# Normed tiles in places of their own, and another order of the seven MLP products, in a two-layer hybrid transformer kernel

## The chip, the cores and the metric

The kernel runs on one NeuronCore of one Trainium2 chip. The metric is the device time of one execution in microseconds (us); lower is better. A profiled execution gives a trace of each engine's instructions: PE (matrix engine), DVE (vector engine), ACT (scalar engine), POOL (the GpSimd engine) and SP (which issues most of the DMAs).

## The reference

Two layers work on x, 512 tokens by 1024 features in float32. Each layer norms x, projects it, mixes it in three ways (retention, sparse attention over keys that an indexer picks, dilated attention), projects back and adds to x; then it norms x again and adds an MLP. A last norm gives the output.

```
for layer in range(2):
    h = rms_norm(x, attn_norm_w[layer])
    proj = h @ w_in[layer]
    mixed = concat(retention(proj), dsa(proj), dilated(proj))
    x = x + mixed @ w_out[layer]
    h = rms_norm(x, mlp_norm_w[layer])
    x = x + square(relu(h @ w_up[layer])) @ w_down[layer]
return rms_norm(x, final_norm_w)
```

Here `rms_norm(x, w) = x * rsqrt(mean(x*x) + 1e-6) * w`, over the 1024 features of one token.

## The kernel before, in words

**Tiles.** x lies in four token tiles t = 0..3 (`xv`, 128 tokens by 1024 features). Every matrix product is made in float32r from a high and a low part of both operands, as three matmuls (high by high, high by low, low by high). A weight is loaded raw by DMA, ACT casts its high part (L277), and DVE or POOL subtracts to get the low part (L285); the pair is a `w` tile, and there are 5 buffers for those.

**A norm of one token tile** (`norm`): POOL multiplies one half of x by the norm's weights (L383), ACT squares and sums both halves (L360), DVE joins the two sums (L363), POOL raises to the power -0.5 (L367), DVE multiplies the first half by that (L387) and makes the second half in one instruction (L390). PE turns each half in 4 transposes (L351, 4 of 128x128 into an `at` bank). From there ACT casts the high part of the activations (L400), and DVE subtracts for the low part (L401), 256 columns at a time. The two normed halves and the two junk outputs of the squares all come from one pool, `P`, of 3 buffers of 128x512, which the sparse attention's small tiles use too.

**Start of a layer.** `token_parts` multiplies the activations of each token tile by a 456-column piece of `w_in` (L347, 24 matmuls for a token tile, 96 in all); then the indexer's matmuls follow (L335 with 128x384). At the start of layer 0 the norm's weights are spread over the partitions by two matmuls into PSUM (L1071), and two copies on ACT (L1086) bring them into a tile `ph` after the norm of tile 2, which reads them in PSUM. `attention` also zeroes two tiles: the retention state `sv` in four DVE instructions (L833) and the low parts of the keys, `KL`, in four POOL ones (L837).

**The MLP** of a layer goes through four stages f = 0..3, each a quarter of the 4096 hidden features: 8 blocks of up-projection (L335, 24 matmuls each), and then the down-projection in seven Strassen-like products P1 to P7. Each product has two parts p = 0, 1 of 12 matmuls of 128x512 (L1032) and two `w` tiles; a first part and a second part add to different token tiles. The products gather in PSUM banks that are not cleared between them (`CHAIN`): P1, P6, P7 and P4 follow each other in the two `rt` banks, P5 and P3 in two `at` banks, P2 stands alone. After each part, one DVE instruction (L1036) adds the bank to half of a token tile of x; the next product of the chain can only write to the bank once that add has read it. P1, P6, P3 and P2 go to tiles 0 and 1, P5, P7 and P4 to tiles 2 and 3; P4 and P2 add to the first half of the features, P6, P7, P5 and P3 to the second. In the last stage of a layer, `finish` starts the norm of a token tile that is complete (layer 0: the next layer's norm; layer 1: `final`, which writes the output).

**What sets the order.** The order on each engine is set before the run by a scheduler that simulates engines and takes a table of priorities; within an engine, instructions run in that order. Weight DMAs are issued ahead by SP as raw buffers come free.

Of the kernel before, what the change touches and what calls it, by code (L numbers as in the profile page):

```python
# [41 lines left out]
PRODUCTS = (("P1", 0), ("P5", 3), ("P6", 4), ("P2", 1), ("P7", 5), ("P3", 6), ("P4", 2))  # L42
# [5 lines left out]
FINISH = ({("P4", 0): (0,), ("P4", 1): (1, 2, 3)},  # L48
          {("P3", 0): (0,), ("P4", 0): (2,), ("P3", 1): (1,), ("P4", 1): (3,)})
# [33 lines left out]
O_PW = O_G + 2  # L83
N_C0 = O_PW + 8
# [9 lines left out]
def constants():  # L94
    f = np.float32
    c = np.zeros((P, N_CST), f)
    i = np.arange(P)
    c[:, O_ID:O_ID + 128] = np.eye(P, dtype=f)
    for k in range(NT):
        d = k * P + i[:, None] - i[None, :]  # L100
        n = ((d >= 0) & (d <= 128)).astype(int) + ((d >= 0) & (d % 4 == 0)) + ((d >= 0) & (d % 16 == 0))
        m = np.where(n > 0, -np.log(np.maximum(n, 1)), BIG)
        o = O_DIL + (NT - 1 - k) * P
        c[:, o:o + P] = m.astype(f)
    d = i[:, None] - i[None, :]
# [12 lines left out]
    c[:, O_PW:O_PW + 8] = -0.5  # L118
    return c
# [7 lines left out]
class Kern:  # L127
    UB = 5

    def __init__(self, nc, tc, ctx, A, out):  # L130
        self.nc, self.tc, self.A, self.out = nc, tc, A, out
        pool = self.pool


        self.psm = pool(ctx, "sm", 9)
        self.p1 = pool(ctx, "const", 1)
        self.pact = pool(ctx, "act", 4)
        self.praw = pool(ctx, "raw", RAWB)
# [215 lines left out]
    def norm_stats(self, t, junk=None, cuts=((0, 512), (512, 1024))):  # L354
# [12 lines left out]
        nc.gpsimd.tensor_tensor(r[:, 0:1], v[:, 0:1], self.c[:, O_PW:O_PW + 1], op=ALU.pow)  # L367
# [7 lines left out]
    def norm(self, t, wb, act, first=False, junk=None, h0=0):  # L375

        nc = self.nc
        hn = [None, None]
        hn[h0] = self.work()
        halves = ((0, 512), (512, 1024))[::1 - 2 * h0]  # L380
        if not first:
            c0, c1 = halves[0]
            nc.gpsimd.tensor_tensor(hn[h0], self.x[t][:, c0:c1], wb[:, c0:c1], op=ALU.mult)  # L383
        r = self.norm_stats(t, junk, halves)
        for h in (h0, 1 - h0):
            if h == h0 and not first:
                nc.vector.tensor_scalar(hn[h], hn[h], r[:, 0:1], None, op0=ALU.mult)  # L387
            else:
                hn[h] = hn[h] or self.work()
                nc.vector.scalar_tensor_tensor(hn[h], self.x[t][:, h * 512:(h + 1) * 512], r[:, 0:1],  # L390
                                               wb[h] if first else wb[:, h * 512:(h + 1) * 512], op0=ALU.mult,
                                               op1=ALU.mult)
            ps = self.at()
            for k in range(4):
                self.tr(ps[:, k * P:(k + 1) * P], hn[h][:, k * P:(k + 1) * P])
# [150 lines left out]
    def token_parts(self, L, act):  # L546
# [5 lines left out]
        for t in (0, 1, 2, 3) if L else (2, 3, 0, 1):  # L552
# [96 lines left out]
    def ret_tile(self, L, t, mix):  # L649
# [83 lines left out]
        nc.gpsimd.tensor_tensor(var[:, 4:8], var[:, 0:4], self.c[:, O_PW:O_PW + 4], op=ALU.pow)  # L733
# [12 lines left out]
    def latent(self, L, c):  # L746
# [10 lines left out]
        nc.gpsimd.tensor_tensor(ss[:, 4:8], ss[:, 0:4], self.c[:, O_PW:O_PW + 4], op=ALU.pow)  # L757
# [65 lines left out]
    def attention(self, L, act):  # L823
# [11 lines left out]
        for z in range(4):  # L835
            o = slice(64, 128) if z % 2 == 0 else slice(0, 64)
            nc.gpsimd.tensor_scalar(self.kl[z // 2][o, z % 2, :], bc(self.ident[o], [[0, 4], [1, P]]), 0.0, 0.0, op0=ALU.mult, op1=ALU.add)  # L837
# [98 lines left out]
        for t in range(NT):  # L936
# [3 lines left out]
            with self.prio("norm", t):  # L940
                self.norm(t, wb, nact)
# [3 lines left out]
    def mlp(self, L, act):  # L945
# [4 lines left out]
        with ExitStack() as ctx:  # L950
# [4 lines left out]
            psw = self.pool(ctx, "wb%d" % L, 1)  # L955

            U = pu.tile([P, 14 * 1024 + 64 * L], F32R, name="U%d" % L)[:, 64 * L:].rearrange("p (j f k c) -> p j f k c", j=2, f=7, k=4)
            for f in range(4):
# [44 lines left out]
                def finish(t):  # L1003
# [4 lines left out]
                    else:  # L1008
                        self.norm(t, wb, nact, h0=t // 2)
# [3 lines left out]
                if L == DEPTH - 1 and last:  # L1013
                    seq[-3:-1] = seq[-2:-4:-1]
                bank = {}
                for key, fac, p in seq:
# [20 lines left out]
                    for t in FINISH[L].get((key, p), ()):  # L1037
                        finish(t)
# [4 lines left out]
    def final(self, t, wb, pool, junk):  # L1043
        nc = self.nc
        h0 = t // 2
        halves = [(0, 512), (512, 1024)][::1 - 2 * h0]
# [3 lines left out]
        r = self.norm_stats(t, junk, halves if t < 3 else halves[:1] + [(d0, d0 + 256), (d0 + 256, d1)])  # L1050
# [6 lines left out]
    def start(self):  # L1057
# [7 lines left out]
        nc.sync.dma_start(self.c[:, :N_C0], self.A["cst"][:, :N_C0])  # L1065
        one = self.work()
# [15 lines left out]
        for t, n in zip((2, 3, 0, 1), PRE):  # L1082
            self.norm(t, wps if t == 2 else wb, act, t == 2)
            if t == 2:
                for h in range(2):
                    nc.scalar.copy(wb[:, h * 512:(h + 1) * 512], wps[h])  # L1086
# [40 lines left out]
```

## Time and profile before

| what | us |
|---|---|
| device time, three runs | 1262.68, 1267.45, 1267.89 (median 1267.45) |
| device time of the profiled execution | 1265.72 |
| span of its trace | 1263.8 |
| PE busy | 1221.3 (97%) |
| DVE busy | 924.7 (73%) |
| ACT busy | 677.6 (54%) |
| POOL busy | 466.6 (37%) |

The span goes from the first to the last instruction in the trace; the device time has a little around it (here 1.92 us). An engine's busy time is summed over the span. Since one engine is busy for almost all of the time, the page's averages say little about the rest: what a change can save is read from the stretches in which that engine stands still or runs slower, and from what it waits for there.

### The profile page before, as it was taken

To read this page: it belongs to the slowest core of one execution; us is meant where nothing else is said; L and a number is where in the kernel's file an instruction comes from. 1 tells how busy PE (TensorE), PEld (TensorE's weight loads), DVE (VectorE), ACT (ScalarE), POOL (GpSimd) and SP (SyncE) were. 2 spreads that over 40 slices of the span, in tenths; PEclk is the share of its full clock that TensorE was granted. 3 is DMA by queue.
4 is the path that set the end of the run, shared out by engine and by line. 5 is a ranking of instruction groups with operands and counts; after the bars stand their busy time and mean duration, and the time that the engine had idled before them with its cause. 6 is when DMAs were issued, how large, how long until landed. Compare 5 with 4: busy or idle time off the path is not lost.

```text
span 1263.8 us, 16891 instructions
## 1 busy us (share of the span) xinstructions
PE 1221.3 (97%) x6116; PEld 1033.1 (82%) x6116; DVE 924.7 (73%) x1589; ACT 677.6 (54%) x1241; POOL 466.6 (37%) x459
## 2 busy tenths in 40 slices
PE   7989999999999999999989999999999999999997
PEld 5978888878888888888879788888798888888886
DVE  6499757856884966858856996586678759578595
ACT  5646558734644535445446465676355445454454
POOL 2444648543411404114024445565444032041232
PEclk9999999999999999999989999999899999999999
DMA  7423223224435062250134232232161531614201
GB/s 211 117 67 92 79 72 118 68 66 130 137 111 157 1 207 59 80 167 16 45 116 134 76 97 71 68 118 66 51 223 45 176 91 44 189 34 140 77 1 67
DMA packets 142180, 122.73 MB, mean 97 GB/s; under 512 B 6801, under 2 KB 114065, under 8 KB 142098
## 3 DMA queue, kind: packets, MB, share of 16 engines
q1 hardware_dynamic: 140178, 118.52, 31.2%
q10 hardware_dynamic: 1920, 3.15, 1.1%
q8 instruction: 48, 0.79, 0.3%
q14 instruction: 34, 0.28, 0.1%
HBM read 114.31 MB, written 4.19 MB: 94 GB/s over the span
## 4 chain that ended last, share of the span: by engine, by line
PE 78%; DVE 15%; ACT 2%; issue 2%; DMA 1%; POOL 1%; SPq 0%; POOLq 0%; DVEq 0%; ACTq 0%
PE mm L335 33%; PE mm L347 14%; PE rt L1032 13%; PE at L1032 9%; DVE sc L604 3%; DVE top L603 3%; PE at L351 2%; PE at L492 2%; PE at L444 1%; PE at L445 1%; DVE ph L463 1%; DVE w L285 1%; DVE Q L425 1%; PE at L335 1%; DVE sc L592 1%
## 5 line engine op out<-in xcount | busy, mean ns | idle before, releaser
L335 PE MATMUL mm<-act,w 128*128 128x512 f32 (+2 forms) x2352 | 514.6, 377 | 3.5 <-DVE Q L425 3.5
L335 PEld LDWEIGHTS mm<-act,w 128*128 128x128 f32 x2352 | 424.2, 188 | 80.6 <-issue 3.0
L285 POOL TENSOR_TENSOR w<-raw,w 128x512 fp32r<-128x512 f32 (+1 forms) x124 | 160.0, 1314 | 86.9 <-ACT w L277 72.0
L1032 PE MATMUL rt<-w,U 128*128 128x512 f32 (+1 forms) x780 | 182.9, 386 | 1.5 <-DVE xv L1036 1.5
L285 DVE TENSOR_TENSOR w<-rd,w 128x1024 fp32r<-128x1024 f32 x112 | 144.6, 1304 | 51.5 <-ACT w L277 51.5
L277 ACT CAST w<-raw 128x1024 fp32r<-128x1024 f32 (+1 forms) x138 | 143.0, 1037 | 72.0 <-PE rt L1032 24.9
L1032 PEld LDWEIGHTS rt<-w,U 128*128 128x128 f32 x780 | 144.9, 188 | 31.2 <-DVE xv L1036 1.7
L277 ACT CAST w<-rd 128x1024 fp32r<-128x1024 f32 x112 | 117.6, 1050 | 94.3 <-PE at L1032 52.5
L285 DVE TENSOR_TENSOR w<-raw,w 128x1024 fp32r<-128x1024 f32 (+1 forms) x76 | 94.5, 1244 | 99.3 <-ACT w L277 99.1
L988 POOL TENSOR_TENSOR st<-s 128x256 f32<-128x256 f32 x32 | 39.1, 1223 | 331.4 <-ACT s L977 325.9
L347 PE MATMUL mm<-w,act 128*128 128x256 f32 (+2 forms) x768 | 144.3, 339 | 8.5 <-ACT xv L525 3.1
L347 PEld LDWEIGHTS mm<-w,act 128*128 128x128 f32 x768 | 120.7, 192 | 24.0 <-ACT xv L525 3.6
L1032 PE MATMUL at<-w,U 128*128 128x512 f32 x576 | 137.4, 389 | 0.0
L1032 PEld LDWEIGHTS at<-w,U 128*128 128x128 f32 x576 | 108.1, 188 | 22.4
L347 PE MATMUL mm<-w,mix 128*128 128x512 f32 x384 | 98.6, 404 | 1.6 <-DVE Q L425 1.1
L303 DVE TENSOR_TENSOR rd<-rd,rd 128x1024 f32<-128x1024 f32 x64 | 94.3, 1473 | 0.6
L975 ACT ACTIVATE s<-mm 128x512 f32<-128x512 f32 x62 | 36.9, 595 | 89.2 <-PE mm L335 79.5
L347 PEld LDWEIGHTS mm<-w,mix 128*128 128x128 f32 x384 | 70.8, 191 | 16.2 <-PE rt L351 1.5
L992 ACT CAST U<-st 128x1024 fp32r<-128x1024 f32 x32 | 33.7, 1053 | 79.7 <-POOL st L989 79.7
L986 POOL TENSOR_TENSOR st<-s,s 128x256 f32<-128x256 f32 x32 | 36.6, 1143 | 92.2 <-ACT s L977 92.2
L993 DVE TENSOR_TENSOR U<-s,U 128x256 fp32r<-128x256 f32 x64 | 63.8, 997 | 0.0
L464 ACT ACTIVATE ph<-ph,sm 128x128 f32<-128x128 f32 (+1 forms) x96 | 53.9, 562 | 16.8 <-DVE sm L463 16.0
(151 smaller groups left out, 1636.0 us busy)
## 6 DMA issues: line engine op xcount, KB each, us to landing
raw<-in_w_up_dram SPq DMA_DIRECT2D x64, 512.0 KB, 4.3
rd<-in_w_down_dram SPq DMA_DIRECT2D x32, 1024.0 KB, 5.1
raw<-in_w_in_dram SPq DMA_DIRECT2D x48, 512.0 KB, 4.0
raw<-in_w_out_dram SPq DMA_DIRECT2D x16, 512.0 KB, 3.8
xv<-in_x_dram SPq DMA_DIRECT2D x7, 512.0 KB, 4.5
KH<-KH ACTq DMA_DIRECT2D x24, 128.0 KB, 2.3
raw<-in_w_in_dram SPq DMA_DIRECT2D x8, 256.0 KB, 3.0
xd<-xv SPq DMA_DIRECT2D x4, 512.0 KB, 6.1
```

The source lines that it names most:

```text
L277: self.nc.scalar.copy(hi, src)
L285: eng.tensor_tensor(lo[:, i:i + step], src[:, i:i + step], hi[:, i:i + step].bitcast(F32), op=ALU.subtract)
L303: sub = lambda o, a, b: self.nc.vector.tensor_tensor(o, a, b, op=ALU.subtract)
L335: self.nc.tensor.matmul(ps[:cols, toks[0]:toks[1]], a, b, start=(k == 0 and j == 0), stop=(k == KB - 1 and j == 2))
L347: self.nc.tensor.matmul(ps[:, :w], a, b, start=(n == 0), stop=(n == tot - 1))
L464: nc.scalar.activation(p, p, AF.Exp, bias=a, scale=-1.0, accum_out=b)
L603: nc.vector.max(m, sc[b])
L604: nc.vector.match_replace(sc[b], m, sc[b], SENT)
L975: nc.scalar.activation(s, ps, AF.Relu)
L988: tt(st[:, 2], a[:, 0], a[:, 1], op=ALU.subtract)
L993: nc.vector.tensor_tensor(lo, src, hi.bitcast(F32), op=ALU.subtract)
L1032: nc.tensor.matmul(ps[:, c0:c1], a, w, start=(new and n == 0), stop=(n == 11), skip_group_check=True)
```

## The change

- The normed halves of a token tile get one tile of their own (`room`): in the attention part and at the start it is a buffer named `KH` or `Q` of the keys' and queries' pool, in the MLP one of a new pool `hn` of 3. Only squares' junk and the sparse attention's small tiles are left in `P`.
- The seven products come in the order P1 P5 P6 P7 P4 P3 P2. Tiles 2 and 3 finish at the two parts of P4, tiles 0 and 1 at those of P2, in both layers. P2 takes two `mm` banks. The last part of all, which is made in two pieces of 256 columns, puts its second piece in a bank of its own.
- The norms at the end of layer 0 start with the second half of the features for each tile (`h0=1`), and layer 1 projects the tiles in the order 2, 3, 0, 1, as layer 0 did.
- The zeroing of `sv` (now one instruction of 128x512) and of `KL` is written behind `token_parts`, all on POOL. The exponent -0.5 is a small tile set by a memset, not a part of the constants' DMA. The two copies of the norm's weights at the start stand ahead of the norms.

The core of the diff:

```diff
-PRODUCTS = (("P1", 0), ("P5", 3), ("P6", 4), ("P2", 1), ("P7", 5), ("P3", 6), ("P4", 2))
+PRODUCTS = (("P1", 0), ("P5", 3), ("P6", 4), ("P7", 5), ("P4", 2), ("P3", 6), ("P2", 1))
-FINISH = ({("P4", 0): (0,), ("P4", 1): (1, 2, 3)},
-          {("P3", 0): (0,), ("P4", 0): (2,), ("P3", 1): (1,), ("P4", 1): (3,)})
+FINISH = {("P4", 0): 2, ("P4", 1): 3, ("P2", 0): 0, ("P2", 1): 1}
...
-    def norm(self, t, wb, act, first=False, junk=None, h0=0):
+    def norm(self, t, wb, act, room, first=False, h0=0):
...
-        hn = [None, None]
-        hn[h0] = self.work()
+        hn = self.t(room[0], [P, 2, S], F32, room[1])
...
-        for t in (0, 1, 2, 3) if L else (2, 3, 0, 1):
+        for t in (2, 3, 0, 1):
...
+    def zeros(self):
+
+        z = lambda o, a: self.nc.gpsimd.tensor_scalar(o, a, 0.0, 0.0, op0=ALU.mult, op1=ALU.add)
+        z(self.sv.rearrange("p a c -> p (a c)"), bc(self.ident, [[0, 4], [1, P]]))
+        for i in range(4):
+            o = slice(64, 128) if i % 2 == 0 else slice(0, 64)
+            z(self.kl[i // 2][o, i % 2, :], bc(self.ident[o], [[0, 4], [1, P]]))
...
-        for z in range(4):
-            nc.vector.tensor_scalar(self.sv[:, z // 2, (z % 2) * P:(z % 2 + 1) * P], self.ident, 0.0, None, op0=ALU.mult)
...
+            if stage == "tv":
+                self.zeros()
...
-                self.norm(t, wb, nact)
+                self.norm(t, wb, nact, (self.pk, "KH" if t < 2 else "Q"))
...
-                        self.norm(t, wb, nact, h0=t // 2)
+                        self.norm(t, wb, nact, (psn, "hn"), h0=1)
...
-                if L == DEPTH - 1 and last:
-                    seq[-3:-1] = seq[-2:-4:-1]
...
-                        bank[b, p] = self.t(self.prt, [P, 512], F32, "rt") if b == "b" else self.at()
+                        bank[b, p] = {"a": self.at, "b": self.rt_bank, "c": self.mm}[b]()
...
+                        ps = self.at() if c0 else ps
...
+        nc.vector.memset(self.pwr, -0.5)
...
+        for h in range(2):
+            nc.scalar.copy(wb[:, h * 512:(h + 1) * 512], wps[h])
```

Where the scheduler moved PE's work. Line numbers differ in the changed kernel: L352 are its transposes, L348 its token products, L1036 its MLP products, L389 and L400 the norm's last scaling and the low parts of the activations. The numbers behind a name tell tiles apart.

At the start of the program, on PE, before: the transposes of tile 2 (`P_143`, `P_163`), 18 token products, then the first transposes of tile 3 (`P_183`).

```order
L351 MATMUL at_154<-cst,P_143 128x128 x4
L351 MATMUL at_165<-cst,P_163 128x128 x4
L347 MATMUL mm_317<-w_176,act_139 128x456 x6
L347 MATMUL mm_317<-w_215,act_140 128x456 x6
L347 MATMUL mm_317<-w_252,act_141 128x456 x6
L351 MATMUL at_195<-cst,P_183 128x128 x4
```

And now: tile 2's (`Q_147`), 2 products, then tile 3's (`Q_184`) and, after 18 more products, those of tile 0 (`KH_220`).

```order
L352 MATMUL at_158<-cst,Q_147 128x128 x4
L352 MATMUL at_168<-cst,Q_147 128x128 x4
L348 MATMUL mm_307<-w_177,act_143 128x456 x2
L352 MATMUL at_196<-cst,Q_184 128x128 x4
L352 MATMUL at_206<-cst,Q_184 128x128 x4
L348 MATMUL mm_307<-w_177,act_143 128x456 x4
L348 MATMUL mm_307<-w_215,act_144 128x456 x6
L348 MATMUL mm_307<-w_251,act_145 128x456 x2
```

Tile 3's transposes moved ahead of 16 of the 18 products.

At the end of layer 0's MLP, on PE, before: the end of P4 (`rt_5517`) with the transposes of tile 0 (`P_5743`) in it, 14 token products of layer 1, then the transposes of tile 1 (`P_5789`); those of tiles 2 and 3 come after 34 further products, one behind the other.

```order
L1032 MATMUL rt_5517<-w_5684,U_3349 128x512 x2
L351 MATMUL at_5755<-cst,P_5743 128x128 x4
L351 MATMUL at_5766<-cst,P_5764 128x128 x4
L1032 MATMUL rt_5517<-w_5684,U_3349 128x512 x4
L347 MATMUL mm_5939<-w_5689,act_5499 128x456 x6
L347 MATMUL mm_5939<-w_5720,act_5500 128x456 x6
L347 MATMUL mm_5939<-w_5725,act_5501 128x456 x2
L351 MATMUL at_5801<-cst,P_5789 128x128 x4
```

And now: P2 (`mm_5786`, `mm_5832`) with the transposes of tile 2 (`hn_5663`) in it, those of tile 3 (`hn_5708`) at its end, and only then token products, 30 of them before the next transposes.

```order
L1036 MATMUL mm_5786<-w_5645,U_3343 128x512 x6
L1036 MATMUL mm_5786<-w_5740,U_3343 128x512 x2
L352 MATMUL at_5675<-cst,hn_5663 128x128 x4
L352 MATMUL at_5685<-cst,hn_5663 128x128 x4
L1036 MATMUL mm_5786<-w_5740,U_3343 128x512 x4
L1036 MATMUL mm_5832<-w_5645,U_3343 128x512 x6
L1036 MATMUL mm_5832<-w_5740,U_3343 128x512 x6
L352 MATMUL at_5720<-cst,hn_5708 128x128 x4
L352 MATMUL at_5730<-cst,hn_5708 128x128 x4
L348 MATMUL mm_5922<-w_5745,act_5493 128x456 x6
```

Two token tiles are normed and turned before layer 1's first product, where it was one.

In the middle of a down-projection (layer 0, f = 0), on PE, now: behind the second part of P6 (`rt_3749`) the first part of P7 (`rt_3735`) takes the bank of P6's first part, then the second part of P7 the bank of P6's second, with matmuls of P3 (`at_3775`, `at_3789`) between them.

```order
L1036 MATMUL rt_3749<-w_3716,U_3343 128x512 x6
L1036 MATMUL rt_3749<-w_3764,U_3343 128x512 x6
L1036 MATMUL rt_3735<-w_3770,U_3343 128x512 x6
L1036 MATMUL rt_3735<-w_3804,U_3343 128x512 x6
L1036 MATMUL at_3775<-w_3847,U_3343 128x512
L1036 MATMUL at_3789<-w_3847,U_3343 128x512
L1036 MATMUL rt_3749<-w_3770,U_3343 128x512 x6
L1036 MATMUL rt_3749<-w_3804,U_3343 128x512 x6
```

Before, the 24 matmuls of P2 stood between P6 and P7.

## Rows read from the trace of the kernel before

**Rows 1.** The page: busy time by engine, share of the span, instructions.

```profile
PE 1221.3 (97%) x6116; PEld 1033.1 (82%) x6116; DVE 924.7 (73%) x1589; ACT 677.6 (54%) x1241; POOL 466.6 (37%) x459
```

**Rows 2.** Windows: stretch, length, busy time by engine, granted PE clock, DMA share, GB/s.

```profile
10.00:30.00 20.00, 17.39 (x80) 13.90 (x80) 15.99 (x28) 13.38 (x38) 5.44 (x6) 1.00 0.74 216
30.00:60.00 30.00, 29.84 (x164) 28.62 (x165) 13.10 (x22) 18.64 (x46) 11.85 (x10) 1.00 0.40 106
606.00:630.00 24.00, 24.00 (x108) 19.87 (x107) 18.41 (x22) 10.63 (x14) 3.11 (x3) 1.00 0.14 43
630.00:655.00 25.00, 19.77 (x92) 16.72 (x91) 16.34 (x34) 13.03 (x43) 6.91 (x10) 0.86 0.53 162
655.00:690.00 35.00, 34.72 (x202) 33.24 (x201) 18.62 (x26) 19.95 (x41) 14.28 (x12) 1.00 0.40 107
```

The engines in these rows are PE, PEld (PE's loading of weights), DVE, ACT and POOL, in this order.

**Rows 3.** Timeline of the start: start, duration, instruction, [idle before <- what ended it].

```profile
5.79 2.69 POOL L837 TENSOR_SCALAR KL<-cst 64x512 fp32r<-64x512 f32 x4 [5.37 <-DMA cst<-in_cst_dram]
...
8.46 1.39 POOL L367 TENSOR_TENSOR sm<-sm,cst 128x1 f32<-128x1 f32 x1
...
10.69 1.97 PE L351 MATMUL at<-cst,P 128*128 128x128 f32 x8 [4.60 <-DMA raw<-in_w_in_dram]
...
12.74 0.65 ACT L360 ACTIVATE P<-xv 128x512 f32<-128x512 f32 x1
...
15.61 0.56 POOL L367 TENSOR_TENSOR sm<-sm,cst 128x1 f32<-128x1 f32 x1 [3.02 <-DVE sm L363]
16.14 1.30 POOL L383 TENSOR_TENSOR P<-xv,ph 128x512 f32<-128x512 f32 x1
16.21 1.52 DVE L387 TENSOR_SCALAR P<-P,sm 128x512 f32<-128x512 f32 x1
...
18.36 1.03 PE L351 MATMUL at<-cst,P 128*128 128x128 f32 x8
...
30.16 10.20 PE L347 MATMUL mm<-w,act 128*128 128x456 f32 x48 [0.29 <-ACT widx L559]
...
40.20 2.09 PE L335 MATMUL mm<-act,w 128*128 128x384 f32 x11
```

**Rows 4.** Line L387: count, shortest, median and longest in ns.

```profile
L387 DVE TENSOR_SCALAR P<-P,sm x15: 472/486/1516, 16.2 to 931.2; 128x512 f32<-128x512 f32 x15
```

**Rows 5.** Timeline of PE, end of layer 0's MLP into layer 1.

```profile
631.97 1.58 PE L347 MATMUL mm<-w,act 128*128 128x456 f32 x6
...
651.36 1.94 PE L351 MATMUL at<-cst,P 128*128 128x128 f32 x8 [3.06 <-DVE P L387]
...
663.76 2.44 PE L335 MATMUL mm<-act,w 128*128 128x384 f32 x13
```

**Rows 6.** Timeline of DVE and PE in a down-projection (layer 0).

```profile
444.34 0.68 DVE L1036 TENSOR_TENSOR xv<-xv,rt 128x512 f32<-128x512 f32 x1
444.93 2.35 DVE L285 TENSOR_TENSOR w<-rd,w 128x1024 fp32r<-128x1024 f32 x2
447.20 0.68 DVE L1036 TENSOR_TENSOR xv<-xv,rt 128x512 f32<-128x512 f32 x1
...
446.11 5.60 PE L1032 MATMUL at<-w,U 128*128 128x512 f32 x24
451.55 5.60 PE L1032 MATMUL rt<-w,U 128*128 128x512 f32 x24
```

**Rows 7.** Timeline of the tail: POOL, DVE, PE.

```profile
1253.48 1.27 POOL L1049 TENSOR_TENSOR s<-xv,wb 128x512 f32<-128x512 f32 x1
...
1253.55 1.75 DVE L1054 SCALAR_TENSOR_TENSOR xv<-xv,sm,wb 128x512 f32<-128x512 f32 x1
...
1257.42 0.42 DVE L1036 TENSOR_TENSOR xv<-xv,rt 128x256 f32<-128x256 f32 x1 [0.30 <-PE rt L1032]
...
1259.36 0.75 DVE L1054 SCALAR_TENSOR_TENSOR xv<-xv,sm,wb 128x512 f32<-128x512 f32 x1 [0.73 <-POOL sm L367]
...
1255.68 1.69 PE L1032 MATMUL rt<-w,U 128*128 128x256 f32 x12 [1.52 <-DVE xv L1036]
```

More of the change, by code (lines that the diff above doesn't have):

```diff
@@ L82 @@
 O_G = O_SCL + 8
-O_PW = O_G + 2
-N_C0 = O_PW + 8
+N_C0 = O_G + 2
 O_COS = N_C0
@@ L117, in constants @@
         c[(h % 2) * 64:(h % 2) * 64 + 64, O_G + h // 2] = np.exp(128.0 * lg)
-    c[:, O_PW:O_PW + 8] = -0.5
     return c
@@ L147, in __init__ @@
         self.ident = self.c[:, O_ID:O_ID + 128]
+        self.pwr = self.p1.tile([P, 8], F32, name="pw")
         self.dram = ctx.enter_context(tc.tile_pool(name="dram", bufs=1, space=bass.MemoryType.DRAM))
@@ L181, in at, with rt_bank @@
         return self.t(self.pat, [P, 512], F32, "at")
+    def rt_bank(self):
+        return self.t(self.prt, [P, 512], F32, "rt")
     def work(self, dt=F32):
@@ L366, in norm_stats @@
         r = self.small()
-        nc.gpsimd.tensor_tensor(r[:, 0:1], v[:, 0:1], self.c[:, O_PW:O_PW + 1], op=ALU.pow)
+        nc.gpsimd.tensor_tensor(r[:, 0:1], v[:, 0:1], self.pwr[:, 0:1], op=ALU.pow)
         return r
@@ L382, in norm @@
             c0, c1 = halves[0]
-            nc.gpsimd.tensor_tensor(hn[h0], self.x[t][:, c0:c1], wb[:, c0:c1], op=ALU.mult)
-        r = self.norm_stats(t, junk, halves)
+            nc.gpsimd.tensor_tensor(hn[:, h0], self.x[t][:, c0:c1], wb[:, c0:c1], op=ALU.mult)
+        r = self.norm_stats(t, None, halves)
         for h in (h0, 1 - h0):
             if h == h0 and not first:
-                nc.vector.tensor_scalar(hn[h], hn[h], r[:, 0:1], None, op0=ALU.mult)
+                nc.vector.tensor_scalar(hn[:, h], hn[:, h], r[:, 0:1], None, op0=ALU.mult)
             else:
-                hn[h] = hn[h] or self.work()
-                nc.vector.scalar_tensor_tensor(hn[h], self.x[t][:, h * 512:(h + 1) * 512], r[:, 0:1],
+                nc.vector.scalar_tensor_tensor(hn[:, h], self.x[t][:, h * 512:(h + 1) * 512], r[:, 0:1],
                                                wb[h] if first else wb[:, h * 512:(h + 1) * 512], op0=ALU.mult,
@@ L394, in norm @@
             for k in range(4):
-                self.tr(ps[:, k * P:(k + 1) * P], hn[h][:, k * P:(k + 1) * P])
+                self.tr(ps[:, k * P:(k + 1) * P], hn[:, h, k * P:(k + 1) * P])
             psv = ps.rearrange("p (k c) -> p k c", k=4)
@@ L831, in attention @@
         self.sv = self.t(self.psc, [P, 2, 4 * HD], F32R, "sv")
-        for z in range(4):
-            nc.vector.tensor_scalar(self.sv[:, z // 2, (z % 2) * P:(z % 2 + 1) * P], self.ident, 0.0, None, op0=ALU.mult)
         self.kl, self.nkl = [self.t(self.psc, [P, 2, S], F32R, "KL%d" % z) for z in range(2)], 0
-        for z in range(4):
-            o = slice(64, 128) if z % 2 == 0 else slice(0, 64)
-            nc.gpsimd.tensor_scalar(self.kl[z // 2][o, z % 2, :], bc(self.ident[o], [[0, 4], [1, P]]), 0.0, 0.0, op0=ALU.mult, op1=ALU.add)
         assert sum(C["TOPK"]) == 16 and sum(C["RET"]) == 12
@@ L955, in mlp @@
             psw = self.pool(ctx, "wb%d" % L, 1)
+            psn = self.pool(ctx, "hn%d" % L, 3)
             U = pu.tile([P, 14 * 1024 + 64 * L], F32R, name="U%d" % L)[:, 64 * L:].rearrange("p (j f k c) -> p j f k c", j=2, f=7, k=4)
@@ L1020, in mlp @@
                     if new:
-                        bank[b, p] = self.t(self.prt, [P, 512], F32, "rt") if b == "b" else self.at()
+                        bank[b, p] = {"a": self.at, "b": self.rt_bank, "c": self.mm}[b]()
                     ps = bank[b, p]
-                    tail = L == DEPTH - 1 and last and (key, p) == ("P4", 1)
+                    tail = L == DEPTH - 1 and last and (key, p) == ("P2", 1)
                     for c0, c1 in ((0, 256), (256, 512)) if tail else ((0, 512),):
+                        ps = self.at() if c0 else ps
                         n = 0
@@ L1036, in mlp @@
                         nc.vector.tensor_tensor(xs, xs, ps[:, c0:c1], op=ALU.add)
-                    for t in FINISH[L].get((key, p), ()):
-                        finish(t)
+                    if (key, p) in FINISH:
+                        finish(FINISH[key, p])
                     if p == 1:
@@ L1044, in final @@
         nc = self.nc
-        h0 = t // 2
-        halves = [(0, 512), (512, 1024)][::1 - 2 * h0]
+        halves = [(512, 1024), (0, 512)]
         (c0, c1), (d0, d1) = halves
@@ L1049, in final @@
         nc.gpsimd.tensor_tensor(xs, self.x[t][:, c0:c1], wb[:, c0:c1], op=ALU.mult)
-        r = self.norm_stats(t, junk, halves if t < 3 else halves[:1] + [(d0, d0 + 256), (d0 + 256, d1)])
+        r = self.norm_stats(t, junk, halves if t != 1 else halves[:1] + [(d0, d0 + 256), (d0 + 256, d1)])
         nc.scalar.activation(xs, xs, AF.Copy, scale=r[:, 0:1])
@@ L1082, in start @@
         for t, n in zip((2, 3, 0, 1), PRE):
[L1083 to L1086, printed above, removed]
+            self.norm(t, wps if t == 2 else wb, act, (self.pk, "KH" if t < 2 else "Q"), t == 2)
             self.done(n)
```

4 lines of the change are left out of this document (2 added, 2 removed).

## Prediction

> **What bounds the kernel now.** I read the page first: PE is busy for 1221.3 of the 1263.8 us of the span [rows 1]. So a change that leaves the matmuls as they are can win back some 42 us at most, in the stretches where PE stands still, and the windows tell which those are [rows 2]. Two of them are touched here. From 10 to 30 us (the norms of the four token tiles at the start) PE works 17.39 of 20 us. From 630 to 655 us (end of layer 0's MLP, norms, first products of layer 1) it works 19.77 of 25, at a granted clock of 0.86, with 1.00 before and after. In the MLP's last 24 us before that PE has no gap at all. PE's timeline there names a reason: at 651.36 its transposes of the last token tile have waited 3.06 us for the normed half that L387 makes [rows 5]. In the tail PE waits 1.52 us for the add that must read a bank before its second piece is written [rows 7].
>
> **Start.** PE reaches the indexer's matmuls (L335) at 40.20. Between its first transposes at 10.69 and there it has 96 token products and 32 transposes to do. Undisturbed, 48 products take 10.20 us, 0.2125 each, and 8 transposes 1.03 [rows 3]: 20.4 + 4.1 = 24.5 us of work in 29.5, so 5.0 us are lost. Tile 3's transposes stand at 18.36, 18 products behind tile 2's; in the new order they come after 2 products, so their input must be early. It can be: the copies of the weights no longer stand behind tile 2's norm, so POOL's product for tile 3 need not wait for it. I follow the chain with durations from [rows 3]. The scheduler leaves the zeroing first on POOL in layer 0: 2.69 us for `KL`, and for `sv` some 0.7 more (an estimate: one of 128x512, where one of 64x512 takes 2.69/4 = 0.67). POOL's first power moves from 8.46 to 9.2 and lasts 1.39 to 10.5, and tile 2's transposes move 0.7 us to 11.4. Then tile 3's product (1.30) ends at 11.8 and its power (0.56) at 12.4, and the products for tiles 0 and 1 follow, to 13.7 and 15.0 if x has landed. L387 beside POOL's product took 1.52 and ended 0.29 us after it [rows 3], where its median is 0.486 [rows 4]; a scaling of L389's kind took 1.75 beside such a product, ending 0.55 after it, and 0.75 alone [rows 7]. So tile 3's halves come at 14.0 and 15.6, and its transposes end at 16.3. Then 94 products and 16 transposes are left, 22.0 us: L335 at 38.3, a gain of 1.9. Were DVE not held by POOL, the halves would come at 12.9 and 13.7 and the gain would be near 4. I take 2.2, nearer to the held case, as both rows show it; bounds 1 (a late tile 0 or 1) and 4.
>
> Here the Trainium skill has a rule (SBUF — State Buffer, "Who interferes with whom"): DVE and GpSimd share a pair of ports as an exclusive lock, and the one that issues second waits until the first has finished. The trace agrees: L387 issued 0.07 us behind L383 and ended 0.29 us after it. By the rule POOL's products in a row hold tile 3's halves one after the other, and the start gains 1.9; without it, about 4.
>
> The other edits of the start I cost at nothing. The memset lies in DVE's first 5 us, when it has no data yet; if that cover were gone it would cost an instruction of 128x8. In layer 1 the zeroing is 3.4 us on POOL behind the last norm's power, and POOL is busy 6.91 of 25 us there [rows 2]; without that cover it would cost these 3.4 us once.
>
> Does a gain at 40 us reach the end? In the 30 us after 30 DVE, which carries the sparse attention's selection that follows, is busy for 13.10, and for 18.62 of the 35 after 655, while PE is full with 29.84 and 34.72 [rows 2]. Both lead into the next stage earlier if PE does, so I take all of it.
>
> **End of layer 0.** From layer 1's first token product (631.97) to L335 (663.76) PE takes 31.8 us [rows 5] for 96 products and 24 transposes (8 lie before): at undisturbed rates 20.4 + 3.1 = 23.5. So 8.3 us are lost there, 5.2 of them as idle time [rows 2], the rest at the lower clock and in short waits. Now token tiles 2 and 3 are complete at P4, and P2's 24 matmuls cover the norms. A matmul of the down-projection takes 0.227 us (24 from 446.11 to 451.55 [rows 6]). Counted back from the end of P2, with 8 transposes in it, P4's first part ends 48 matmuls ahead (11.9 us) and its second 31 ahead (8.1). A norm behind that needs the add (0.68 [rows 6]), two squares (0.65 each and their sums, 1.6), the power (0.56 and the join, 0.7), L387 (1.52 at worst) and L389 (0.75): 5.3 us. Tile 2's transposes are due 4.7 us before the end: slack 1.9. Tile 3's are due at the end: slack 2.8. Tiles 0 and 1 end 2.7 and 0 us before it and are due 7.4 and 10 us after: slack near 5. DVE is busy 18.41 of 24 us in that stretch [rows 2], so one low part of 1.2 us (half of the 2.35 of two [rows 6]) can stand ahead of the norm at each place and still fit. The ideal is 632.0 + 23.5 = 655.5, a gain of 8.3. I take 7.5, as some short waits will stay; bounds 5 (one norm comes 3 us too late) and 8.3.
>
> **MLP in between.** Its other stages I cost at 0, with the time between an add and the next write to its bank as cover. P7's first part now takes the bank of P6's first, whose add runs from 444.34 to 444.93, and PE ends P6 at 446.11 [rows 6]: 1.2 us of cover. P7's second part starts 14 matmuls later, at 449.3, and its bank is read at 447.9: 1.4 us. Before, the 5.44 us of P2 lay between as well. DVE's queue has pairs of low parts of 2.35 us [rows 6]; with one moved ahead of such an add PE stands still for 1.2 and 0.95 us. There is nothing to gain, as PE has no gap. Bounds 0 and 2.1 us a stage; I take 0, since DVE's order puts each add ahead of the low parts that are cast at the same time, as in [rows 6].
>
> **Tail.** The second piece has its own bank, which removes PE's wait of 1.52 us. But the last add (1257.42) also stands behind other tiles' scalings in DVE's order, one of which took 1.75 beside POOL's product [rows 7]; it should come about 0.7 us sooner. Bounds: 1.0 worse (one more such scaling in front), 1.4 better (the whole wait).
>
> **Sum.** 2.2 + 7.5 + 0 + 0.7 = 10.4. The profiled execution took 1265.72 and would take 1255.3. It lies 1.7 us below the runs' median of 1267.45; I count from halfway between the two, 1266.6, and predict **1256.2**. With the lower bounds (1 + 5 - 1 = 5) it is 1261.6, with the upper (4 + 8.3 + 1.4 = 13.7) 1252.9.
>
> **Rivals.**
> - *Half the gain.* Tile 2's or 3's norm comes late at the end of layer 0. For: DVE at 77%, and four norms now share it with P2's adds. Against: slacks of 1.9 and more. If only the one wait of 3.06 us [rows 5] and the start's lower bound and the tail are won, 3.1 + 1 + 0.7 = 4.8: 1261.8.
> - *It doesn't do what it says.* The three `P` buffers never held a norm up, since L387 waits for POOL's power in any case; the norms' pace comes from ACT, POOL and DVE in turn, which places of their own don't change, and it stays the pace of PE's transposes. Then some 2 us at the start and the tail are left: 1264.6.
> - *Slower: P7 on P6's heels.* In each of the 8 down-projections a pair of low parts gets ahead of P6's adds: 2.1 us each, 17 us in all, and 1256.2 + 17 = 1273. For: the cover shrinks by 5.44 us to 1.2. Against: [rows 6] has the adds first. From 1.3 us a stage on it eats the whole gain.
>
> **How the numbers follow.** Forecast 0.58, half the gain 0.18, nothing 0.12, slower 0.12. A difference of 0.5%, 6.3 us, is about what can be told here (the three runs lie 5.2 apart). The forecast's own range, 1251 to 1261, is all faster; half the gain lies at the border (0.06 faster, 0.12 same); nothing is the same; of the slower case 0.02 is within 0.5%. Faster 0.64, same 0.26, slower 0.10. The range from 1251.0 (the upper bounds, and the 1.7 us between run and median) to 1265.0 leaves out the slower case and a little beside.
>
> **What would show it.** In the changed trace: layer 0's L335 at about 38, with tile 3's transposes right behind tile 2's; PE full around layer 1's start at a clock of 1.00, and L335 some 23.5 to 24.5 us after P2's end; no wait of PE for L1036's adds at P7; no wait before the last piece. I am wrong if PE waits for an add at the first matmul of P7 or P4, if tile 2's or 3's transposes at the end of layer 0 wait for L387 or L389, or if the selection starts no earlier.

## The result and the profile after

The changed kernel took 1252.55 us (median of 1252.02, 1250.14, 1253.53 and 1253.09), the kernel before 1267.65 in the same comparison: a ratio of 0.9887, with a 95% interval of 0.9859 to 0.9916. In a second comparison it took 1256.04 against 1267.39, 0.9900 (0.9877 to 0.9923). The forecast was 1256.2 with a range of 1251.0 to 1265.0. The span of the profiled execution fell from 1263.8 to 1250.0 us, by 13.8.

The page of the changed kernel, busy time by engine; it answers to [rows 1]:

```profile
PE 1216.8 (97%) x6116; PEld 1031.2 (82%) x6116; DVE 915.4 (73%) x1582; ACT 680.1 (54%) x1241; POOL 474.7 (38%) x461
```

PE's share rounds to 97% in both kernels: its busy time fell by 4.5 us and the time in which it stands still from 42.5 to 33.2 us. Where the time went is seen in the windows of the changed kernel at the two places of [rows 2]:

```profile
10.00:30.00 20.00, 18.53 (x89) 16.23 (x90) 16.40 (x31) 14.06 (x40) 6.85 (x7) 1.00 0.73 216
606.00:630.00 24.00, 24.00 (x111) 19.94 (x110) 19.44 (x24) 13.39 (x22) 8.74 (x6) 1.00 0.28 89
630.00:655.00 25.00, 24.49 (x130) 21.86 (x129) 15.22 (x29) 14.44 (x46) 4.92 (x8) 1.00 0.46 132
```

From 630 to 655 us PE now works 24.49 of 25 us, where it was 19.77, and the granted clock is 1.00 (2.4 GHz), where it was 0.86. PE's timeline of the changed kernel at the same place answers to [rows 5]:

```profile
625.69 1.03 PE L352 MATMUL at<-cst,hn 128*128 128x128 f32 x8
626.48 3.92 PE L1036 MATMUL mm<-w,U 128*128 128x512 f32 x16
630.24 1.03 PE L352 MATMUL at<-cst,hn 128*128 128x128 f32 x8
631.03 2.03 PE L348 MATMUL mm<-w,act 128*128 128x456 f32 x8
633.57 4.81 PE L348 MATMUL mm<-w,act 128*128 128x456 f32 x22 [0.51 <-DVE act L400]
...
641.55 12.25 PE L348 MATMUL mm<-w,act 128*128 128x456 f32 x58
653.64 7.47 PE L336 MATMUL mm<-act,w 128*128 128x384 f32 x42
```

Two tiles are turned by the end of P2, one short wait of 0.51 is left, and the indexer starts at 653.64, 23.4 us after 630.24, where the first instruction behind P2 begins. In the kernel before the same stretch took 31.8 us.

For a ledger I cut the program at places that every kernel has: the indexer's first matmul in layer 0 and in layer 1, and the start of the last down-projection in each. All are read off PE's timeline.

| stretch, us | before | changed | changed, second profile |
|---|---|---|---|
| start to indexer, layer 0 | 40.20 | 38.17 | 39.21 |
| attention, layer 0, with the first up-projection | 307.99 | 308.26 | 309.33 |
| MLP, layer 0, from the first to the last down-projection | 244.80 | 244.80 | 244.80 |
| last down-projection to indexer, layer 1 | 70.77 | 62.41 | 62.42 |
| attention, layer 1, with the first up-projection | 308.65 | 306.37 | 310.84 |
| MLP, layer 1, from the first to the last down-projection | 244.80 | 244.80 | 244.80 |
| last down-projection to the end | 46.6 | 45.2 | 45.2 |
| span | 1263.8 | 1250.0 | 1256.6 |

The stretches that the change touches give 2.0, 8.4 and 1.4 us. The two attention stretches differ by up to 4.5 us between two executions of one and the same kernel, which the experiments go into.

### The profile page after: what moved, and what is told of

It reads as the page before. It is cut to its first block, busy times and chain, and to the rows that moved or that the text cites. A ratio compares the mean times of both kernels' runs of the same rounds, so it can differ in the third digit from the quotient of the medians.

```text
span 1250.0 us, 16890 instructions
## 1 busy us (share of the span) xinstructions
PE 1216.8 (97%) x6116; PEld 1031.2 (82%) x6116; DVE 915.4 (73%) x1582; ACT 680.1 (54%) x1241; POOL 474.7 (38%) x461
## 4 chain that ended last, share of the span: by engine, by line
PE 83%; DVE 13%; ACT 2%; issue 1%; DMA 0%; SPq 0%; POOL 0%; POOLq 0%; DVEq 0%; ACTq 0%
PE mm L336 34%; PE mm L348 15%; PE rt L1036 14%; PE at L1036 7%; DVE sc L603 3%; PE mm L1036 3%; DVE top L602 3%; PE at L352 2%; PE at L491 2%; PE at L443 1%; PE at L444 1%; PE at L336 1%; DVE ph L462 1%; PE rt L690 1%; DVE Q L424 1%
## 5 line engine op out<-in xcount | busy, mean ns | idle before, releaser
L1036 PE MATMUL rt<-w,U 128*128 128x512 f32 x768 | 183.2, 389 | 0.0
L1036 PEld LDWEIGHTS rt<-w,U 128*128 128x128 f32 x768 | 144.2, 188 | 29.9
L348 PE MATMUL mm<-w,act 128*128 128x256 f32 (+2 forms) x768 | 142.7, 336 | 5.6 <-ACT xv L524 3.1
L348 PEld LDWEIGHTS mm<-w,act 128*128 128x128 f32 x768 | 119.4, 191 | 18.7 <-ACT xv L524 3.6
L348 PE MATMUL mm<-w,mix 128*128 128x512 f32 x384 | 99.4, 406 | 1.6 <-DVE Q L424 1.1
L1036 PE MATMUL at<-w,U 128*128 128x512 f32 (+1 forms) x396 | 97.7, 386 | 0.0
L1036 PEld LDWEIGHTS at<-w,U 128*128 128x128 f32 x396 | 73.6, 188 | 15.0
L348 PEld LDWEIGHTS mm<-w,mix 128*128 128x128 f32 x384 | 71.5, 193 | 16.3 <-PE rt L352 1.5
```

The costliest lines, as they stand in the source:

```text
L348: self.nc.tensor.matmul(ps[:, :w], a, b, start=(n == 0), stop=(n == tot - 1))
L1036: nc.tensor.matmul(ps[:, c0:c1], a, w, start=(new and n == 0), stop=(n == 11), skip_group_check=True)
```

## The experiments

The start of layer 0's last down-projection to layer 1's indexer is called the boundary below: 70.77 us before, 62.41 after.

**The order alone, and the places alone.** Two kernels, each with one half of the change made in the kernel before. `e1_order` has the products' order, their banks, the tail and the tiles' order:

```diff
-PRODUCTS = (("P1", 0), ("P5", 3), ("P6", 4), ("P2", 1), ("P7", 5), ("P3", 6), ("P4", 2))
+PRODUCTS = (("P1", 0), ("P5", 3), ("P6", 4), ("P7", 5), ("P4", 2), ("P3", 6), ("P2", 1))
...
+FINISH = {("P4", 0): 2, ("P4", 1): 3, ("P2", 0): 0, ("P2", 1): 1}
...
+                        bank[b, p] = {"a": self.at, "b": self.rt_bank, "c": self.mm}[b]()
...
```

> The kernel before with the new order of products alone (P1 P5 P6 P7 P4 P3 P2, tiles finishing at P4 and P2, P2 in its own banks, the tail's second bank, norms starting with the second half); normed halves stay in the three shared buffers, start and zeroing as before. Theory A (the order gives the norms P2 as cover): from the end of the down-projection of layer 0 to the indexer's first matmul 24 to 26 us, where before took 31.8 and the changed kernel 23.4, and 7 to 10 us less than before in all. Theory B (the places do it): the stretch stays at 29 us or more, and the time within 3 us of before, the tail's 1 us included.

`e2_places` has the tiles of their own and nothing else:

```diff
-        hn = [None, None]
-        hn[h0] = self.work()
+        hn = self.t(room[0], [P, 2, S], F32, room[1])
...
+                        self.norm(t, wb, nact, (psn, "hn"), h0=t // 2)
...
```

> The kernel before with places of their own for the normed halves alone; order of products, start and zeroing as before. Theory A (cover by P2): the norms of three of the four tiles still begin at the end of P4, so the stretch from the end of the down-projection to the indexer stays at 28 us or more; in all 0 to 4 us less than before, the start included. Theory B (buffers held the norms up): the stretch falls to 25 us or less and the time by 7 us or more.

The order alone took 1257.72 us against 1267.96 (ratio 0.9923, 0.9908 to 0.9939), the places alone 1256.90 (0.9913, 0.9894 to 0.9931). The boundary is 65.87 us with the order and 64.15 with the places. From the end of the down-projection to the indexer that is some 27 us with the order, where theory A had 24 to 26, and 25 with the places, theory B's limit. So each half works without the other: they bring 4.9 and 6.6 of the 8.4 us, and together they don't add up, since both remove the same loss. With the order alone PE works 23.09 of the 25 us from 630 to 655, at a granted clock of 0.93; with the places alone 23.41, at 1.00. How the places do it, POOL's timeline of the kernel with places alone shows (line L382 is the first product of a norm, L367 its power):

```profile
612.65 1.29 POOL L382 TENSOR_TENSOR hn<-xv,wb 128x512 f32<-128x512 f32 x1 [13.52 <-DVE xv L1035]
615.37 2.20 POOL L382 TENSOR_TENSOR hn<-xv,wb 128x512 f32<-128x512 f32 x1 [1.43 <-DVE xv L1035]
619.33 1.30 POOL L382 TENSOR_TENSOR hn<-xv,wb 128x512 f32<-128x512 f32 x1 [1.76 <-DVE xv L1035]
624.95 0.55 POOL L367 TENSOR_TENSOR sm<-sm,cst 128x1 f32<-128x1 f32 x1 [4.32 <-DVE sm L363]
630.07 0.55 POOL L367 TENSOR_TENSOR sm<-sm,cst 128x1 f32<-128x1 f32 x1 [4.57 <-DVE sm L363]
```

And the kernel before, the same place:

```profile
624.83 0.55 POOL L367 TENSOR_TENSOR sm<-sm,cst 128x1 f32<-128x1 f32 x1 [10.53 <-DVE sm L363]
625.34 1.29 POOL L383 TENSOR_TENSOR P<-xv,wb 128x512 f32<-128x512 f32 x1
633.13 0.55 POOL L367 TENSOR_TENSOR sm<-sm,cst 128x1 f32<-128x1 f32 x1 [6.49 <-DVE sm L363]
633.65 1.28 POOL L383 TENSOR_TENSOR P<-xv,wb 128x512 f32<-128x512 f32 x1
```

With three shared buffers each norm's first product came only behind the power of the norm before it, one every 8 us. With places of their own three products are made before the first power, and the norms overlap. So the buffers did hold the norms up.

**The copies at the start.** The changed kernel with the two copies put back behind tile 2's norm.

```diff
-        for h in range(2):
-            nc.scalar.copy(wb[:, h * 512:(h + 1) * 512], wps[h])
...
+            if t == 2:
+                for h in range(2):
+                    nc.scalar.copy(wb[:, h * 512:(h + 1) * 512], wps[h])
```

> The changed kernel with the two copies of the norm's weights put back behind the norm of tile 2. Theory A (the early copies made the start's gain): layer 0's indexer starts at 40 to 41 us instead of 38.2, and the wait of 1.1 us in front of the query and key products at 110 us that fell away comes back too: 2 to 3 us more. Theory B (places of their own for tile 3's halves made it): the start stays at 38 to 39 us, and 0 to 1 us more in all.

The indexer started at 38.94, 0.8 us later than in the first profile of the changed kernel and 0.3 earlier than in its second. For the start theory B holds: the places made most of the gain (places alone 38.88, order alone 39.93, one profile each). What the copies add can't be told, as 38.94 lies between the changed kernel's two profiles. The time was 1257.95 (0.9927, 0.9910 to 0.9944), 2 to 5 us above the changed kernel's two medians, which is not B's 0 to 1, and the waits of 1.1 us were there again; I took that for theory A's second half, until the next profile.

**The changed kernel again.**

> The changed kernel once more, with a second profile. Theory A (what moves in the attention between kernels with the same order of instructions is set by a race of two engines for some hundredths of a us and by the clock, and can fall either way from one execution to the next): of the two three-instruction mask additions, 0.69 us each in the first profile and 1.77 in the kernel before, at least one may come out at 1.77, with a PE wait of 1.1 us behind it; the spells of lower clock may lie elsewhere; the span moves by 1 to 4 us. Theory B (the change itself ended those waits): both come out at 0.69 again and the span lies within 1 us of 1250.0.

Theory A holds, though the span moved by 6.6 us, more than its 1 to 4. The first profile of the changed kernel has, of DVE's mask additions (L593) and POOL's subtraction beside them:

```profile
73.00 2.07 POOL L526 TENSOR_TENSOR xv<-P,xv 128x256 fp32r<-128x256 f32 x2 [10.24 <-ACT xv L524]
...
73.08 0.69 DVE L593 SCALAR_TENSOR_TENSOR sc<-masks,sc 128x128 f32<-128x128 f32 x3
```

The second profile of the same kernel, with PE's wait behind it:

```profile
74.05 1.51 POOL L526 TENSOR_TENSOR xv<-P,xv 128x256 fp32r<-128x256 f32 x2 [10.26 <-ACT xv L524]
...
74.13 1.77 DVE L593 SCALAR_TENSOR_TENSOR sc<-masks,sc 128x128 f32<-128x128 f32 x3
...
92.04 5.69 PE L336 MATMUL mm<-act,w 128*128 128x512 f32 x24 [1.10 <-DVE Q L424]
```

Both times DVE's row begins 0.08 us behind POOL's. Once the additions take 0.69 and POOL's pair 2.07; the other time 1.77 and 1.51, and then PE waits 1.1 us for the queries some 16 us later. Layer 1 fell the same way as layer 0 in each of these profiles. The kernel before and all other experiments that kept this pair had 1.77 or 1.78 in both layers, ten of eleven profiles in all. This is worth 2.2 us for the two layers, and the first profile of the changed kernel had it by luck. The Trainium skill (SBUF — State Buffer, "Who interferes with whom") says that issue order decides which engine is held; the trace agrees that one of the two is held for 0.56 (2.07 to 1.51) or 1.08 us, but its time stamps are too close to say who was first.

The other difference is the granted clock. Windows of 860 to 915 us, first and second profile of the changed kernel:

```profile
860.00:915.00 55.00, 51.85 (x276) 42.83 (x275) 36.36 (x77) 26.13 (x59) 26.38 (x28) 0.97 0.22 63
```

```profile
860.00:915.00 55.00, 51.86 (x260) 42.91 (x259) 32.89 (x73) 23.48 (x54) 26.62 (x29) 0.91 0.17 50
```

PE is as busy, but at a mean clock of 0.91 where it had 0.97 (part of the stretch at 1.2 GHz); 0.06 of 55 us is 3.3 us, which with the 1.1 us above makes up 4.4 of the 4.5 us between the two profiles in layer 1's attention. In the kernel before the clock was 0.94 there.

**No race.** The changed kernel with the first two subtractions of that kind on DVE, straight from PSUM.

```diff
-        self.evac_v(ps, 4, self.vd[g, t // 2][:, t % 2, :], True)
+        self.evac_v(ps, 4, self.vd[g, t // 2][:, t % 2, :], not (g == 0 and t < 2))
```

> The changed kernel with the low parts of the first two dilated value blocks made on DVE straight from PSUM, not on POOL from a copy, so that POOL has no two-input instruction beside the three mask additions. Theory A (which of the two engines takes the turn there decides 1.1 us a layer, and it falls differently from one execution to the next): the three mask additions take 0.7 to 0.9 us in both layers, PE's waits of 1.1 us behind them are gone or half as long, DVE has 0.8 us more to do, and the time is 0 to 2 us below that of the changed kernel where its additions took 1.77. Theory B (the additions are slow for another reason): 1.77 again.

The additions took 0.29, 0.29 and 0.58:

```profile
74.78 0.74 POOL L526 TENSOR_TENSOR xv<-P,xv 128x256 fp32r<-128x256 f32 x1 [12.30 <-ACT xv L524]
...
74.28 0.29 DVE L593 SCALAR_TENSOR_TENSOR sc<-masks,sc 128x128 f32<-128x128 f32 x1
...
75.09 0.58 DVE L593 SCALAR_TENSOR_TENSOR sc<-masks,sc 128x128 f32<-128x128 f32 x1
```

The first two have no POOL instruction beside them; the third began within POOL's next subtraction of this kind, and it alone is longer. So theory A's cause stands. But PE's waits behind them did not go: there are now two of 2.2 us where four had 3.5 in all, as DVE has the subtractions too. 1252.05 us against 1265.25 (0.9896, 0.9860 to 0.9933) can't be told from the changed kernel.

**P2 back between P6 and P7, and P2 in the transposes' banks.** `e4_cover` gives P7 its distance from P6 again; `e11_p2_at` keeps the order and changes the pool.

```diff
-("P6", 4), ("P7", 5), ("P4", 2), ("P3", 6), ("P2", 1))
+("P6", 4), ("P2", 1), ("P7", 5), ("P4", 2), ("P3", 6))
...
-FINISH = {("P4", 0): 2, ("P4", 1): 3, ("P2", 0): 0, ("P2", 1): 1}
+FINISH = {("P4", 0): 2, ("P4", 1): 3, ("P3", 0): 0, ("P3", 1): 1}
...
```

> The changed kernel with P2 back between P6 and P7 (P1 P5 P6 P2 P7 P4 P3), so that P7 no longer follows P6 on its banks; tiles 0 and 1 finish at P3, and the last part has one bank. Theory A (1.2 us of cover is enough for the add): the inner stages take as long as in the changed kernel, 38.1 us a down-projection, and the whole time differs by 0 to 2 us, the tail's 1 us included. Theory B (P7 on P6's heels costs a few tenths to 2 us a stage): each down-projection is shorter by that, 2 us or more in all.

It took 1263.72 us (0.9972, 0.9960 to 0.9985), 8 to 11 us more than the changed kernel's two medians, which neither theory had. The question it was made for is answered: from the first to the last down-projection of a layer every kernel here takes 244.80 us, with P2 between and without, so P7 on P6's heels costs nothing. What it lost is at the boundary, 68.60 us, and some in the tail (48.1). Its timeline at the boundary, PE and one row of DVE:

```profile
621.63 2.88 PE L1036 MATMUL rt<-w,U 128*128 128x512 f32 x12
624.35 1.30 PE L1036 MATMUL at<-w,U 128*128 128x512 f32 x5
625.48 2.88 PE L1036 MATMUL rt<-w,U 128*128 128x512 f32 x12
628.20 1.98 PE L1036 MATMUL at<-w,U 128*128 128x512 f32 x8
630.02 1.03 PE L352 MATMUL at<-cst,hn 128*128 128x128 f32 x8
635.54 1.13 PE L348 MATMUL mm<-w,act 128*128 128x456 f32 x2 [4.49 <-ACT act L399]
...
628.28 0.74 DVE L389 SCALAR_TENSOR_TENSOR hn<-xv,sm,wb 128x512 f32<-128x512 f32 x1
```

P3 (`at`) runs mixed with the two parts of P4 (`rt`): 25 of its and P4's matmuls follow P4's first part and 8 its second, where the changed kernel has 48 and 31. So P3 covers the norms for much less time than P2 did. Tile 2's transposes start only when P3 has ended, 1 us after its normed halves were ready at 629.02, and PE then stands 4.49 us for the casts behind them. P3 also gathers in two of the four `at` banks, from which the transposes take theirs. To see what such banks cost, P2 was put there in the changed order:

```diff
-                        bank[b, p] = {"a": self.at, "b": self.rt_bank, "c": self.mm}[b]()
+                        bank[b, p] = {"a": self.at, "b": self.rt_bank, "c": self.at}[b]()
```

> The changed kernel with P2 in two at banks, the pool from which the transposes take theirs, instead of mm banks. Theory A (the last product has to leave the transposes' banks free, which is why P3 in the last place did not cover the norms): from the start of layer 0's last down-projection to the indexer 65 us or more, where the changed kernel takes 62.4 and the one before 70.7. Theory B (banks don't matter; the place of P3 as the second part's chain does): 62 to 63.5 us.

PE's timeline of its one run (1263.13 us):

```profile
621.39 1.75 PE L1036 MATMUL at<-w,U 128*128 128x512 f32 x7
622.98 1.03 PE L352 MATMUL at<-cst,hn 128*128 128x128 f32 x8
627.78 0.76 PE L348 MATMUL mm<-w,act 128*128 128x456 f32 x2 [3.77 <-ACT act L399]
628.93 1.97 PE L352 MATMUL at<-cst,hn 128*128 128x128 f32 x8 [0.39 <-DVE hn L387]
630.55 3.52 PE L1036 MATMUL at<-w,U 128*128 128x512 f32 x12
```

The boundary is 70.18 us, almost all of the gain gone, and 6 us longer than with the places alone in the old order. P2's first part now runs behind the transposes of tiles 2 and 3 (630.55) and covers nothing; PE stands 3.77 us before that, until tile 2's activations are cast. So the cover is P2 in banks that the norms don't use. For P3 in the last place its mixing with P4 is seen above; what its banks cost besides was not separated.

**Slow norms.** The changed kernel with four more scalings of 128x512 in each norm at the end of layer 0.

```diff
+        if room[1] == "hn":
+            for _ in range(4):
+                nc.vector.scalar_tensor_tensor(hn[:, 1 - h0], self.x[t][:, 0:512], r[:, 0:1], wb[:, 0:512], op0=ALU.mult, op1=ALU.mult)
```

> The changed kernel with four more scalings of 128x512 on DVE in each norm at the end of layer 0 (3.0 us a tile, 12 us of DVE in all; they write what the real one then overwrites). Theory A (the norms are covered with 1.9 us and more of slack by P2, and DVE has room): the stretch from the end of the down-projection to the indexer grows from 23.4 to 25 to 28 us. Theory B (the norms' pace sets the stretch): it grows by about 12 us, to 35.

The boundary took 71.51 us, 9.1 more and longer than in the kernel before, and the time of the one run was 1263.34. Window of that kernel:

```profile
630.00:655.00 25.00, 20.42 (x93) 16.98 (x94) 19.68 (x38) 9.39 (x30) 5.55 (x8) 0.86 0.39 117
```

Neither expectation is met, and B is nearer. PE lost 4.6 us there as idle time (25 less 20.42), where it was 0.5 in the changed kernel, and the clock fell to 0.86 as before the change: 0.14 of 25 us is 3.5 us more. Another wait of 1.2 us lies just ahead of the window. So of 12 us on DVE some 5 became waits of PE, to which the clock added 3.5, and 6 to 7 were covered. The slacks of 1.9 to 5 us that I gave each norm are not one for each: they share one DVE.

**One bank in the tail.**

```diff
-                        ps = self.at() if c0 else ps
```

> The changed kernel with one bank for both pieces of the last part, as before. Theory A (the second bank removes the wait for the add): PE waits 1.5 us before its last 12 matmuls again, and the end comes 0.7 to 1.5 us later. Theory B (the last add is held up by DVE's other work anyway): the end moves by less than 0.4 us.

From the start of the last down-projection to the end it took 45.6 us, against 45.2 with two banks and 46.6 before. The add of the first piece and PE's second piece, in the kernel before and in this one:

```profile
1255.22 0.41 DVE L1036 TENSOR_TENSOR xv<-xv,rt 128x256 f32<-128x256 f32 x1
```

```profile
1247.00 0.42 DVE L1039 TENSOR_TENSOR xv<-xv,mm 128x256 f32<-128x256 f32 x1 [0.74 <-PE mm L1035]
...
1247.48 1.69 PE L1035 MATMUL mm<-w,U 128*128 128x256 f32 x12 [0.51 <-DVE xv L1039]
```

Before, the add came right behind the scaling of 1.75 us of [rows 7]; now DVE stands idle until PE is done, and PE waits 0.51 us, not 1.52. So the order saves 1.0 us of that wait (with the places alone the stretch stayed at 46.6), and the second bank the last 0.4. That is at theory B's limit. The time was 1255.76 (0.9913, 0.9886 to 0.9939).

**Zeroing behind the powers.** In the changed kernel POOL still zeroes first in layer 0, as the constants from which the zeros are made land early. Made from the masks, they come later:

```diff
-        z(self.sv.rearrange("p a c -> p (a c)"), bc(self.ident, [[0, 4], [1, P]]))
+        m = self.masks[:, O_CAUS - N_C1:O_CAUS - N_C1 + P]
+        z(self.sv.rearrange("p a c -> p (a c)"), bc(m, [[0, 4], [1, P]]))
...
-            z(self.kl[i // 2][o, i % 2, :], bc(self.ident[o], [[0, 4], [1, P]]))
+            z(self.kl[i // 2][o, i % 2, :], bc(m[o], [[0, 4], [1, P]]))
```

> The changed kernel with the zeroed tiles made from the masks, which land later, instead of the first constants, so that the order puts the zeroing behind all four powers on POOL in layer 0 too (in the changed kernel it is still first). Theory A (the zeroing ahead of the first power delays tile 2's transposes, but the landing of x for tiles 0, 1 and 3 sets the rest): transposes of tile 2 at about 8 us instead of 11.0, the indexer 0 to 1.5 us earlier than 38.2. Theory B (the zeroing sets the start's length): the indexer 3 us earlier.

The first four transposes were issued at 6.89, the next four at 9.98, and the indexer's first matmul at 36.61, 1.6 us earlier than in the changed kernel's first profile (the changed start lay between 37.6 and 39.2 in the profiles that have it). 1254.24 us (0.9896, 0.9881 to 0.9910). That is theory A, just above its range and far from B's 3 us. POOL's products there wait 3.50 and 2.00 us for x to land, as theory A has it; it was not tried apart. Both of the last edits together:

> The changed kernel with the zeroing made from the masks, behind the powers, and with the first two dilated value blocks' low parts on DVE. Theory A (start and mask additions are independent of each other): layer 0's indexer at 36.6 us, the mask additions at 0.9 us or less, and 2 to 3 us less than the changed kernel, near 1251. Theory B (what the start gains is given back at the selection, which DVE sets): no less than 1253.

1250.60 us against 1265.25 (0.9881, 0.9859 to 0.9904), the indexer at 36.14: the lowest median here, though its interval overlaps with the changed kernel's.

## Why the prediction was right, step by step

- **Start, 2.2 (bounds 1 and 4):** 2.0 and 1.0 in the two profiles, by two paths. The second profile took the path of my sum, with POOL's products beside tile 3's scalings:

```profile
12.79 2.67 POOL L383 TENSOR_TENSOR KH<-xv,ph 128x512 f32<-128x512 f32 x2
...
12.85 1.49 DVE L387 TENSOR_SCALAR Q<-Q,sm 128x512 f32<-128x512 f32 x1 [0.45 <-POOL sm L368]
14.26 1.75 DVE L389 SCALAR_TENSOR_TENSOR Q<-xv,sm,ph 128x512 f32<-128x512 f32 x1
...
16.07 1.11 PE L352 MATMUL at<-cst,Q 128*128 128x128 f32 x4 [0.56 <-DVE Q L389]
```

  Tile 3's halves came at 14.3 and 16.0 (14.0 and 15.6 in the sum), its transposes ended at 17.2 (16.3), and the indexer started at 39.21, where the sum had 38.3. In the first profile POOL's products for tiles 0 and 1 had to wait for x, as the timeline shows for DVE, POOL and PE:

```profile
13.31 0.48 DVE L387 TENSOR_SCALAR Q<-Q,sm 128x512 f32<-128x512 f32 x1
...
13.92 3.77 POOL L383 TENSOR_TENSOR KH<-xv,ph 128x512 f32<-128x512 f32 x2 [1.59 <-DMA xv<-in_x_dram]
...
13.85 1.97 PE L352 MATMUL at<-cst,Q 128*128 128x128 f32 x8
```

  So tile 3's halves were not held by POOL (0.48 instead of 1.52) and its transposes ended at 15.8. Yet the gain was 2.0 and not the 4 that I gave this case: a low part of 1.11 us (12.29 on DVE) stood in front of the scalings, and PE waited 0.35 us for another one later. Of the seven profiles that have this start, six went this way, with the indexer at 37.6 to 38.2. That 2.2 fits is in part luck: neither path gave what I had for it, and the choice between them is made by when x lands. I also gave the credit to the copies, and the places alone had most of it.
- **End of layer 0, 7.5 (5 to 8.3):** 8.4, the whole loss of 8.3 within the reading. That the lost clock would come back with PE's idle time was right: 1.00 for 0.86, in every profile where PE worked 24.49 of the 25 us. P2's cover, which I gave the whole gain, is one of two causes, as places of their own bring 6.6 us without it. And the slacks of the four norms, counted one by one, share one DVE.
- **MLP in between, 0:** 0.00 in both layers. The add of P6's first part stood in front of the low parts as in [rows 6], and PE never waited for one. (The row of that add ends at 445.02, not at the 444.93 that I read, so the cover is 1.1 us; nothing changes by it.)
- **Tail, 0.7 (-1.0 to 1.4):** 1.4, the upper bound: the whole wait is gone. The second bank is 0.4 of it, and the order of the products the rest, as the add no longer stands behind another tile's scaling. I had the whole gain in the bank and expected such a scaling to take half of it back.
- **Sum, 10.4:** the four terms measured 2.0 + 8.4 + 0 + 1.4 = 11.8 in the first profile and 10.8 in the second. The rest of the first profile's 13.8 is 2.2 us for DVE's turn beside POOL; the clock in the two attentions about evened out. In the second profile the clock took 3.4 us back, and the span fell by 7.2 only. So one kernel's span moves by 6.6 us from one execution to the next, and its two medians, 1252.55 and 1256.04, lie 3.7 us below the forecast and on it: the time bears the forecast out only to within some 4 us, and the stretches say more.
- **The rivals:** "doesn't do what it says" was wrong in its reason. Places of their own alone gave 6.6 us at the boundary. "Half the gain" did not come either; with 12 us more on DVE the whole gain of the boundary was gone, and no smaller delay was tried. P7 on P6's heels costs nothing here. What I had not priced was P2's banks: with the `at` pool the gain would have been 0.6 us at the boundary.

## What to carry to other kernels

The tail of a loop covers the start of the next stage only as far as it holds none of the buffers and banks that this stage starts with: with P2 in the transposes' banks the same order kept 0.6 of 8.4 us, less than the old order with places of their own. It must also really come last: P3 was last in the program, and its matmuls ran between those of P4. Two edits that remove one and the same stall don't add up, so each is to be tried alone before either gets the credit. And where DVE and POOL each have two-input work at the same moment, one profile can show a gain or a loss of 1 us that the next profile of the same kernel does not have: take a second profile before a difference of that size is explained.

## What the hardware showed

The turn of DVE and POOL at the mask additions fell differently in two executions of the same program, with the same 0.08 us between their starts: 0.69 and 2.07 us, or 1.77 and 1.51. With no POOL instruction beside it one such addition took 0.29 us. At the start the same scaling of 128x512 on DVE took 1.49 us beside POOL's product in one execution and 0.48 in the other, where x landed later and the product began behind it. The mean granted clock of one and the same stretch (860 to 915 us) was 0.97 in one execution of the changed kernel and 0.91 in the other, with PE busy for 51.85 and 51.86 us.
